# A hybrid decoder step: accumulating decode output, dtx on GpSimd, C's taps a tick later, and paired py and state bursts in the SSD mixer

## The chip, the core and the metric

The kernel runs on one core of a Trainium2 chip. The metric is the device time of one execution in microseconds (us): the median of three runs. The engines are named as the profile names them: PE is TensorE (PEld its weight loads), DVE is VectorE, ACT is ScalarE, POOL is GpSimd, and SP is the queue that issues the transfers.

## What is computed

The reference is one inference step of a trunk of two layers for 256 prompt tokens and 8 decode tokens (one for each of 8 sequences with a state). In each layer three mixers read the same normed input through one input projection, and their outputs go through one output projection. The change lies in the third mixer, the state space one (SSD), with 32 heads of 64 channels, 4 groups of heads and a state of 128 entries per channel:

```
xbc_c, ssm_conv_new = _causal_conv(xbc, ssm_buf, ssm_w, ssm_b)      # 4 taps
xs, bm, cm = split(silu(xbc_c))                                     # x, B, C
dt = softplus(dt + dt_bias); A = -exp(a_log); a = dt * A
# in a chunk of the prompt, per head:
acum = cumsum(a); lmat = exp(acum_i - acum_j) for i >= j, else 0
y = ((C B^T) * lmat * dt_j) x  + (C s) * exp(acum)
s = exp(last) * s + (B * wj)^T x,   wj = exp(last - acum) * dt
# a decode token, per sequence:
s = exp(a) * s + (dt * x) B^T;      y = s C
y = y + d_skip * x
o_ssm = rmsnorm(y * silu(z))
```

The outputs are the two token streams and the new states of all mixers.

## The kernel before

**Tiling.** Channels lie on the 128 partitions and the 264 tokens (`T`: 256 of the prompt, 8 decode) along the free dimension. The SSD channels make 16 channel tiles `ct` of 128 (two heads each); four of them, c = 0 to 3, form a group `g` that shares B and C.

**Projections.** `gemm` (lines 162 to 215) multiplies the weights with the activations. Weights come from memory in pieces of 128 x 1024, four pieces to a projection of 256 columns. Each piece is split into a high part `whi` (ScalarE, line 136) and a low part `wlo` (VectorE, line 129), and each 128 x 128 block is used in three matmuls (line 211): whi with the high and the low activations, wlo with the high ones. So a piece is 24 matmuls and a projection 96. `issue` (line 120) makes the parts ahead of their use, and issues the loads up to six pieces ahead.

**The order of the work.** The order on every compute engine is the order of the program. The small work of the mixers is written as generators. `start` puts one in a list, and `tick` (line 148), called after each piece of a projection, lets every generator in the list run to its next `yield`, the older ones first. A tick is thus as long as 24 matmuls and what the generators add on PE. `yield n` sleeps n ticks. Beside it there is a list `weave`: what is put there runs between the steps of an `in_turn` (line 326) when that has one chain left, otherwise at the end of the tick.

**A group.** `group` (line 652) makes B and C of a group: it fills two tiles from PSUM, starts the convolution on ScalarE (`tap0`), empties the weave, runs the six remaining taps of B and C in turn in one tick on VectorE (lines 663 and 323), then tanh and `cv_silu`, the transposes and the spreading of B and C of the decode tokens over the partitions (`bb`, `cc`).

**A channel tile.** `ssd` (line 691) does one `ct`. Counting its ticks from 0: (0) it loads the decode state `st` (128 x 8 x 128) and evacuates x and z; (1) tap 0 and the gate's tanh; (2) three taps, and half of the states' decay on ScalarE; (3) tanh, gate, the other half; (4) `cv_silu`, `dtx` = x dt for the 8 decode tokens on VectorE (line 719), and the decay matrices `lm` on ScalarE; (5) half of the outer products dtx B into `u` on ScalarE (line 738); (6) the transposes of x, the other half, and the products `lm` x CB, put into the weave; (7) `xdt` (its tile is `vt`, line 749), `xw` (`kt`), the new state st + u (line 752) and its store; (8) PE's burst `py` (lines 757 and 760), and u = st x cc (line 761); (9) PE's burst `pn` for the new prompt state (line 765), y of the prompt (line 768), and the decode output `yd` as the reduction of u (line 770); (10) the copy of pn, stored for each second tile, y of the decode tokens, and the product with the gate on GpSimd (line 778); (12) and (13) the high and low parts of y (lines 781 and 788) and its square, summed up on GpSimd (line 790). As a projection has four ticks, three or four tiles are in flight at a time.

**Buffers.** `tl(tag, shape, bufs)` takes the next of `bufs` buffers of a tag and waits for its last reader. Tags are shared among stages: `x`, `gate` and `lm` have 3 buffers, `sq` has 5, `u` has 1.

Of the kernel before, what the change touches and what calls it, by code (L numbers as in the profile page):

```python
# [19 lines left out]
NB = 8  # L20
# [13 lines left out]
def hybrid_step(ctx, tc, a, depth=DEPTH):  # L34
# [304 lines left out]
    def layer(l, last, ssq_in, between, sq_in):  # L339
# [24 lines left out]
        so = {}  # L364
# [29 lines left out]
        def ret_qk(h, d, psq, psk):  # L394
# [10 lines left out]
            for ps, tag in ((psq, "conv"), (psk, "x")):  # L405
                x1 = tl(tag, [128, T], 3 if tag == "x" else 2)
# [19 lines left out]
            d["pp"] = pp = tl("lm", [128, 384], 3)  # L426
# [7 lines left out]
        def ret_vg(h, d, psv, psg):  # L434
            v = tl("x", [128, T], 3)
# [5 lines left out]
            gate = tl("gate", [128, T], 3)  # L441
# [34 lines left out]
            on = tl("lm", [128, 3, 128], 3)  # L476
# [19 lines left out]
        def sc_prep(c, d):  # L496
            d["ext"] = ext = tl("x", [128, W], 3)
# [17 lines left out]
        def sc_b(c, d, slot, psbg, psg):  # L515
# [5 lines left out]
            gate = tl("gate", [128, T], 3)  # L521
# [6 lines left out]
            m = tl("og", [128, T], 2)  # L528
# [25 lines left out]
        def dt_path(pdt):  # L554
# [10 lines left out]
            rl = tl("x", [128, T], 3)  # L565
# [6 lines left out]
            s1 = tl("x", [128, T], 3)  # L572
# [46 lines left out]
            ac = tl("lm", [128, 384], 3)[32:64, :256]  # L619
# [12 lines left out]
        def cv_prep(ct, tag="x", bufs=3):  # L632
# [19 lines left out]
        def group(g, d, eb, ec, psb, psc):  # L652
# [38 lines left out]
        def ssd(ct, d, ext, psx, psz, ssq):  # L691
# [14 lines left out]
            gate = tl("gate", [128, T], 3)  # L706
# [12 lines left out]
            V.tensor_mul(dtx, xd, dex[:, ct, 0:NB])  # L719
            lms = []  # L720
            for hh in range(2):
                h = 2 * ct + hh
                lm = tl("lm", [128, 384], 3)
# [28 lines left out]
            V.tensor_add(st, st, u)  # L752
            nc.sync.dma_start(a["ssm_state_out"][l, ct], st)
            yield
            py = psm()
            for hh in range(2):
                PE.matmul(py[64 * hh:64 * hh + 64, :256].rearrange("p (b i) -> p b i", b=2), xdt[:, 0, hh],  # L757
                          lms[hh].rearrange("p (b i) -> p b i", b=3)[:, 0:3:2], start=True, stop=False)
            for hh in range(2):
                PE.matmul(py[64 * hh:64 * hh + 64, 128:256], xdt[:, 1, hh], lms[hh][:, 128:256], start=False, stop=True)  # L760
            V.tensor_mul(u, st, d["cc"])
            yield
            pn = psm()
            for j in range(2):
                PE.matmul(pn[:, :128], xw[:, j].rearrange("p h c -> p (h c)"), d["bt"][:, j], start=(j == 0), stop=(j == 1))  # L765
# [4 lines left out]
            V.tensor_reduce(yd, u, axis=mybir.AxisListType.X, op=ALU.add)  # L770
# [11 lines left out]
            if ct:  # L782
                sq = tl("sq", [128, T], 5)
# [95 lines left out]
        for tag, bufs, n in (("st", 3, 3), ("st", 3, 3), ("st", 3, 3), ("bc0", 1, 3), ("bc1", 1, 3), ("gate", 3, 1)):  # L879
# [6 lines left out]
        def evac_a(c, pss, hurry=False):  # L886
            for i, ps in enumerate(pss):
                for j in range(2):
# [7 lines left out]
                    sq = tl("sq", [128, T], 5)  # L896
# [79 lines left out]
    def feed(l, dst, scaled, update, sums=None):  # L976
# [14 lines left out]
        def square(ct):  # L991
            x = acc[:, ct]
            if update:
                squares[ct] = tl("sq", [128, T], 5)
# [3 lines left out]
            else:  # L998
                sq = tl("sq", [128, T], 5)
# [234 lines left out]
```

## Time and profile before

| what | value |
|---|---|
| median of 3 runs (lowest to highest) | 1759.31 us (1759.02 to 1759.42) |
| the profiled execution | 1760.18 us, its span 1758.4 us |
| granted PE clock | 0.999 of full speed |
| first layer's SSD stage, 94.9 to 358.0 us of the span | PE 260.09 us of 263.10, DVE 248.59, ACT 225.22, POOL 69.96 |

The span runs from the first to the last instruction; the profiled execution's own time holds a little more. Busy times count the time in which at least one instruction of an engine is under way. Matmuls overlap, so what one costs is read from the starts of two neighbours, not from its duration. In a timeline row stand the start, the duration, the engine and line, the operation, the tile written and the tiles read, the shape and how many neighbouring instructions the row merges; in square brackets stands the idle time just before it and what ended it. In a row of a group of instructions stand the shapes and the count, then the busy time in us, the mean of one in ns, and the idle time before them.

### The profile page before, as it was taken

The page shows a single profiled execution, that of the slowest core. Times are in us where ns is not written, and L with a number is a line of the kernel's source. Part 1 is how long each engine was busy: PE and PEld are TensorE (multiplying, and loading weights), DVE is VectorE, ACT ScalarE, POOL GpSimd, SP SyncE. Part 2 cuts the span into 40 slices and gives each one's busy share as a digit, 9 for nine tenths or more (in the row PEclk, how much of TensorE's full clock was granted, in tenths as well). Part 3 has the DMA queues.
Part 4 walks back from the last instruction along what each step waited for, and adds up shares of the span by engine and source line. Part 5 has one row for each costly group of instructions (what it writes and reads, how often), then busy time and mean ns, then how long its engine had stood idle before and what let it go on. Part 6 is the DMA issues. An engine that isn't in the chain of part 4 may idle for free.

```text
span 1758.4 us, 36846 instructions
## 1 busy us (share of the span) xinstructions
PE 1735.6 (99%) x14364; PEld 1705.7 (97%) x14364; DVE 1332.2 (76%) x2410; ACT 1010.0 (57%) x1976; POOL 333.5 (19%) x478
## 2 busy tenths in 40 slices
PE   8999999999999999999999999999999999999997
PEld 8999999999999999999999999999999999999997
DVE  7889999974588787554588999999646788765554
ACT  6488888843344444444565888888434444444453
POOL 4213233220021021101202133222102111111022
PEclk9999999999999999999999999999999999999999
DMA  7677787776676766555566777787656777666553
GB/s 276 219 247 249 239 270 249 259 231 180 192 224 210 232 224 211 179 187 180 181 190 212 258 251 241 264 259 247 218 181 186 226 232 218 215 210 183 185 180 104
DMA packets 115487, 382.34 MB, mean 217 GB/s; under 512 B 13872, under 2 KB 21104, under 8 KB 115312
## 3 DMA queue, kind: packets, MB, share of 16 engines
q1 hardware_dynamic: 114880, 378.91, 67.7%
q8 instruction: 112, 1.84, 0.4%
q10 hardware_dynamic: 432, 1.08, 0.2%
q14 instruction: 63, 0.52, 0.1%
HBM read 346.29 MB, written 33.64 MB: 216 GB/s over the span
## 4 chain that ended last, share of the span: by engine, by line
PE 94%; DVE 4%; DMA 1%; issue 1%; ACT 0%; SPq 0%; DVEq 0%; ACTq 0%
PE pj L211 86%; DVE wlo L129 1%; PE m L211 1%; PE m L757 1%; PE m L312 1%; PE m L765 1%; PE m L464 1%; DVE yd L770 0%; DVE conv L323 0%; PE m L422 0%; PE m L760 0%; PE m L482 0%; DVE acc L949 0%; PE pj L386 0%; DMA acc<-x 0%
## 5 line engine op out<-in xcount | busy, mean ns | idle before, releaser
L129 DVE TENSOR_TENSOR wlo<-raw,whi 128x1024 fp32r<-128x1024 f32 x544 | 678.4, 1248 | 321.7 <-issue 160.1
L136 ACT CAST whi<-raw 128x1024 fp32r<-128x1024 f32 x543 | 567.4, 1045 | 601.5 <-PE pj L211 527.7
L211 PE MATMUL pj<-hhi,whi 128*128 128x264 f32 x3256 | 835.9, 290 | 6.5 <-ACT whi L1036 6.0
L211 PE MATMUL pj<-hlo,whi 128*128 128x264 f32 x3256 | 813.2, 286 | 0.0
L211 PEld LDWEIGHTS pj<-hhi,whi 128*128 128x128 f32 x3256 | 613.8, 189 | 17.7 <-issue 6.6
L211 PEld LDWEIGHTS pj<-hlo,whi 128*128 128x128 f32 x3256 | 613.2, 189 | 0.1
L211 PE MATMUL pj<-hhi,wlo 128*128 128x264 f32 x3256 | 485.8, 285 | 0.0
L211 PEld LDWEIGHTS pj<-hhi,wlo 128*128 128x128 f32 x3256 | 433.5, 189 | 0.0
L211 PE MATMUL pj<-mh,whi 128*128 128x264 f32 x1024 | 256.5, 285 | 0.0
L211 PE MATMUL pj<-ml,whi 128*128 128x264 f32 x1024 | 255.8, 285 | 0.0
L211 PEld LDWEIGHTS pj<-mh,whi 128*128 128x128 f32 x1024 | 192.8, 188 | 0.4 <-ACT whi L136 0.3
L211 PEld LDWEIGHTS pj<-ml,whi 128*128 128x128 f32 x1024 | 193.0, 188 | 0.1
L211 PE MATMUL pj<-mh,wlo 128*128 128x264 f32 x1024 | 149.3, 284 | 0.0
L211 PEld LDWEIGHTS pj<-mh,wlo 128*128 128x128 f32 x1024 | 135.0, 188 | 0.0
L738 ACT ACTIVATE u<-bc,dtx 128x128 f32<-128x128 f32 x256 | 82.0, 392 | 37.0 <-DVE yd L770 37.0
L414 POOL TENSOR_TENSOR conv<-conv,rope 128x264 f32<-128x264 f32 x16 | 12.1, 759 | 437.5 <-DVE rope L410 396.4
L702 ACT ACTIVATE st<-st,dex 128x128 f32<-128x128 f32 x256 | 81.2, 389 | 0.0
L323 DVE SCALAR_TENSOR_TENSOR conv<-x,par,conv 128x288 f32<-128x288 f32 (+1 forms) x128 | 68.4, 534 | 14.7 <-ACT conv L317 13.7
L790 POOL TENSOR_TENSOR ssq<-ssq,sq 128x264 f32<-128x264 f32 x30 | 45.3, 1511 | 163.1 <-ACT sq L784 138.6
L903 POOL TENSOR_TENSOR ssq<-ssq,sq 128x264 f32<-128x264 f32 x28 | 30.4, 1086 | 157.4 <-ACT sq L897 157.2
L778 POOL TENSOR_TENSOR og<-og,gate 128x264 f32<-128x264 f32 x32 | 32.2, 1006 | 101.9 <-DVE og L777 95.3
L509 POOL COPY scst<-x 128x16 f32<-128x16 f32 x16 | 13.4, 839 | 190.0 <-DVE x L507 146.4
(314 smaller groups left out, 1665.9 us busy)
## 6 DMA issues: line engine op xcount, KB each, us to landing
raw<-w_in SPq DMA_DIRECT2D x415, 512.0 KB
raw<-w_out SPq DMA_DIRECT2D x128, 512.0 KB
st<-ssm_state SPq DMA_DIRECT2D x32, 512.0 KB
bc<-rows SPq DMA_DIRECT2D x32, 512.0 KB
ssm_state_out<-st SPq DMA_DIRECT2D x32, 512.0 KB
abc<-acum SPq DMA_DIRECT2D x32, 256.0 KB
st<-ret_state SPq DMA_DIRECT2D x16, 512.0 KB
ret_state_out<-st SPq DMA_DIRECT2D x16, 512.0 KB
```

Source lines behind the costliest of these rows:

```text
L129: V.tensor_sub(lo, raw, hi.bitcast(F32))
L136: S.copy(hi, loaded[p])
L211: PE.matmul(ps[gi][c][:, :T], w[:, kk, c * 128:c * 128 + 128], r[half], start=(w is hi and half == 0 and kk + q == 0), stop=(q == 3 and kk ...
L312: PE.transpose(pt[:, j * 128:j * 128 + 128], src[:, j * 128:j * 128 + 128], ident)
L323: V.scalar_tensor_tensor(o[:, :n], ext[:, j:j + n], par[:, c:c + 1], o[:, :n], op0=ALU.mult, op1=ALU.add)
L464: PE.matmul(pd[p0:p0 + 32, :128], qm[:, b], st[:, b], start=(b < 4), stop=(b >= 4))
L702: S.activation(st[:, b], st[:, b], AF.Copy, scale=dex[:, ct, NB + b:NB + b + 1])
L738: S.activation(u[:, b], d["bb"][:, b], AF.Copy, scale=dtx[:, b:b + 1])
L757: PE.matmul(py[64 * hh:64 * hh + 64, :256].rearrange("p (b i) -> p b i", b=2), xdt[:, 0, hh], lms[hh].rearrange("p (b i) -> p b i", b=3)[: ...
L778: G.tensor_mul(y, y, gate)
L790: G.tensor_add(ssq, ssq, sq)
L903: G.tensor_add(ssq2, ssq2, sq)
```

## The change

It does five things.

- **Decode output.** The multiply of 128 x 1024 (line 761) and the reduction (line 770) become eight `scalar_tensor_tensor`, one for each decode token, 128 x 128 each, that multiply the state with cc and put the sum of the products into a column of `yd` through `accum_out`. Four are in tick 8 and four in tick 9.
- **New state.** The addition st + u and the store go into the weave of tick 7.
- **dtx** goes from VectorE to GpSimd.
- **Pairs.** An even tile keeps its `xdt`, `xw` and `lm`. The odd tile that follows runs py for both into one PSUM tile, and a tick later pn for both into another, which one copy evacuates. The even tile's y and what follows it come four ticks later.
- **C's taps.** `group` runs B's taps in one tick, with the weave between them, and C's taps in the next, beside B's tanh; C's tanh goes a tick later. The loop that empties the weave first is gone.

Buffers go with it: `x`, `gate` and `lm` get 4 buffers, `sq` 2. The product `m` of the short convolution moves from `og` to `lm`, and two of three squares that the second layer's first projection reads move from `sq` to `lm`.

```diff
         def group(g, d, eb, ec, psb, psc):
...
             yield
-            while weave:
-                woven()
-            in_turn(taps(ob, eb, 288, 4, P_SW, 16 + g, 24, par), taps(oc, ec, 288, 4, P_SW, 20 + g, 24, par))
+            in_turn(taps(ob, eb, 288, 4, P_SW, 16 + g, 24, par))
             B, C = eb, ec
             yield
             S.activation(B[:, :288], ob[:, :288], AF.Tanh)
+            in_turn(taps(oc, ec, 288, 4, P_SW, 20 + g, 24, par))
+            yield
             S.activation(C[:, :288], oc[:, :288], AF.Tanh)
-            yield
             cv_silu(B, ob)
...
             dtx = tl("dtx", [128, NB], 2)
-            V.tensor_mul(dtx, xd, dex[:, ct, 0:NB])
+            G.tensor_mul(dtx, xd, dex[:, ct, 0:NB])
...
-            V.tensor_add(st, st, u)
-            nc.sync.dma_start(a["ssm_state_out"][l, ct], st)
-            yield
-            py = psm()
-            for hh in range(2):
-                PE.matmul(py[64 * hh:64 * hh + 64, :256].rearrange("p (b i) -> p b i", b=2), xdt[:, 0, hh],
-                          lms[hh].rearrange("p (b i) -> p b i", b=3)[:, 0:3:2], start=True, stop=False)
-            for hh in range(2):
-                PE.matmul(py[64 * hh:64 * hh + 64, 128:256], xdt[:, 1, hh], lms[hh][:, 128:256], start=False, stop=True)
-            V.tensor_mul(u, st, d["cc"])
-            yield
-            pn = psm()
-            for j in range(2):
-                PE.matmul(pn[:, :128], xw[:, j].rearrange("p h c -> p (h c)"), d["bt"][:, j], start=(j == 0), stop=(j == 1))
+
+            def new_state():
+                V.tensor_add(st, st, u)
+                nc.sync.dma_start(a["ssm_state_out"][l, ct], st)
+
+            weave.append(new_state)
+            yield
+            pair.append((xdt, xw, lms))
+            if ct % 2:
+                both = psm()
+                for i, (xt, _, ls) in enumerate(pair):
+                    pi = both[:, 256 * i:256 * i + 256]
+                    for hh in range(2):
+                        PE.matmul(pi[64 * hh:64 * hh + 64].rearrange("p (b i) -> p b i", b=2), xt[:, 0, hh],
+                                  ls[hh].rearrange("p (b i) -> p b i", b=3)[:, 0:3:2], start=True, stop=False)
+                    for hh in range(2):
+                        PE.matmul(pi[64 * hh:64 * hh + 64, 128:256], xt[:, 1, hh], ls[hh][:, 128:256], start=False, stop=True)
+                pys[ct - 1], pys[ct] = both[:, :256], both[:, 256:]
+            yd = tl("yd", [128, NB], 2)
+
+            def decode(bs):
+                for b in bs:
+                    V.scalar_tensor_tensor(u[:, b], st[:, b], 1.0, d["cc"][:, b], op0=ALU.mult, op1=ALU.mult,
+                                           accum_out=yd[:, b:b + 1])
+
+            decode(range(0, 4))
+            yield
+            if ct % 2:
+                pn = psm()
+                for i, (_, xs, _) in enumerate(pair):
+                    for j in range(2):
+                        PE.matmul(pn[:, 128 * i:128 * i + 128], xs[:, j].rearrange("p h c -> p (h c)"), d["bt"][:, j],
+                                  start=(j == 0), stop=(j == 1))
+                pair.clear()
+            decode(range(4, NB))
+            if ct % 2 == 0:
+                yield 4
             y = tl("og", [128, T], 2)
             dsk = par[:, P_DSK + ct:P_DSK + ct + 1]
-            V.scalar_tensor_tensor(y[:, :TP], x[:, :TP], dsk, py[:, :TP], op0=ALU.mult, op1=ALU.add)
-            yd = tl("yd", [128, NB], 2)
-            V.tensor_reduce(yd, u, axis=mybir.AxisListType.X, op=ALU.add)
-            yield
-            if ct % 2 == 0:
-                so[0] = tl("so", [128, 2, 128], 2)
-            S.copy(so[0][:, ct % 2], pn[:, :128])
-            if ct % 2 == 1:
-                nc.sync.dma_start(a["ssm_new"][l, ct // 2], so[0])
+            V.scalar_tensor_tensor(y[:, :TP], x[:, :TP], dsk, pys.pop(ct), op0=ALU.mult, op1=ALU.add)
+            yield
+            if ct % 2:
+                so = tl("so", [128, 2, 128], 2)
+                S.copy(so.rearrange("p j n -> p (j n)"), pn[:, :256])
+                nc.sync.dma_start(a["ssm_new"][l, ct // 2], so)
             V.scalar_tensor_tensor(y[:, TP:T], xd, dsk, yd, op0=ALU.mult, op1=ALU.add)
             G.tensor_mul(y, y, gate)
```

More of the change, by code (lines that the diff above doesn't have):

```diff
@@ L362, in hr @@
             return hhi[:, k], hlo[:, k]
-        so = {}
+        pair, pys = [], {}
         rot_t = []
@@ L425, in ret_qk @@
             yield
-            d["pp"] = pp = tl("lm", [128, 384], 3)
+            d["pp"] = pp = tl("lm", [128, 384], 4)
             V.tensor_mul(pp[:, :256], psc[:, :256], dm)
@@ L434, in ret_vg @@
         def ret_vg(h, d, psv, psg):
-            v = tl("x", [128, T], 3)
+            v = tl("x", [128, T], 4)
             V.tensor_mul(v, psv[:, :T], r2)
@@ L440, in ret_vg @@
             st, kt, pp, qm = d["st"], d["kt"], d["pp"], d["qm"]
-            gate = tl("gate", [128, T], 3)
+            gate = tl("gate", [128, T], 4)
             S.activation(gate, pre, AF.Tanh, scale=0.5)
@@ L475, in ret_vg @@
             yield
-            on = tl("lm", [128, 3, 128], 3)
+            on = tl("lm", [128, 3, 128], 4)
             for j in range(3):
@@ L496, in sc_prep @@
         def sc_prep(c, d):
-            d["ext"] = ext = tl("x", [128, W], 3)
+            d["ext"] = ext = tl("x", [128, W], 4)
             G.memset(ext[:, 0:2], 0.0)
@@ L520, in sc_b @@
             yield
-            gate = tl("gate", [128, T], 3)
+            gate = tl("gate", [128, T], 4)
             S.activation(gate, pre, AF.Tanh, scale=0.5)
@@ L527, in sc_b @@
             cv = d["cv"]
-            m = tl("og", [128, T], 2)
+            m = tl("lm", [128, 384], 4)[:, :T]
             G.tensor_mul(m[:, :TP], cv[:, :TP], bg[:, :TP])
@@ L564, in dt_path @@
             dtb = par[:, P_DTB:P_DTB + 1]
-            rl = tl("x", [128, T], 3)
+            rl = tl("x", [128, T], 4)
             S.activation(rl, d0, AF.Relu, bias=dtb)
@@ L571, in dt_path @@
             yield
-            s1 = tl("x", [128, T], 3)
+            s1 = tl("x", [128, T], 4)
             V.tensor_scalar(s1, d0, 2.0, None, op0=ALU.add)
@@ L618, in dt_path @@
             yield
-            ac = tl("lm", [128, 384], 3)[32:64, :256]
+            ac = tl("lm", [128, 384], 4)[32:64, :256]
             V.tensor_copy(ac, pa[32:64, :256])
@@ L705, in ssd @@
             o = tap0(ext, 288, P_SW, ct, P_SB, par)
-            gate = tl("gate", [128, T], 3)
+            gate = tl("gate", [128, T], 4)
             S.activation(gate, pre, AF.Tanh, scale=0.5)
@@ L722, in ssd @@
                 h = 2 * ct + hh
-                lm = tl("lm", [128, 384], 3)
+                lm = tl("lm", [128, 384], 4)
                 ab = abc_t[ct][:, hh]
@@ L782, in ssd @@
             if ct:
-                sq = tl("sq", [128, T], 5)
+                sq = tl("sq", [128, T], 2)
                 S.activation(sq, y, AF.Square)
@@ L878, in layer @@
         xres, xparts = [], []
-        for tag, bufs, n in (("st", 3, 3), ("st", 3, 3), ("st", 3, 3), ("bc0", 1, 3), ("bc1", 1, 3), ("gate", 3, 1)):
+        for tag, bufs, n in (("st", 3, 3), ("st", 3, 3), ("st", 3, 3), ("bc0", 1, 3), ("bc1", 1, 3), ("gate", 4, 1)):
             t = tl(tag, [128, n, T], bufs)
@@ L895, in evac_a @@
                         yield
-                    sq = tl("sq", [128, T], 5)
+                    sq = tl("sq", [128, T], 2)
                     S.activation(sq, acc[:, ct], AF.Square)
@@ L993, in square @@
             if update:
-                squares[ct] = tl("sq", [128, T], 5)
+                squares[ct] = tl("sq", [128, T], 2) if ct % 3 == 2 else tl("lm", [128, 384], 4)[:, :T]
                 S.activation(squares[ct], x, AF.Square)
@@ L998, in square @@
             else:
-                sq = tl("sq", [128, T], 5)
+                sq = tl("sq", [128, T], 2)
                 S.activation(sq, x, AF.Square)
```

4 lines of the change are left out of this document (2 added, 2 removed).

## The prediction

> **What bounds the kernel now.** I read the page first, then the list of waits of TensorE, then its timeline around the SSD bursts, then VectorE in the same stretch.
>
> ```profile
> span 1758.4 us, 36846 instructions
> PE 1735.6 (99%) x14364; PEld 1705.7 (97%) x14364; DVE 1332.2 (76%) x2410; ACT 1010.0 (57%) x1976; POOL 333.5 (19%) x478
> DVE  7889999974588787554588999999646788765554
> PE m L757 <- DVE vt L749: 6.1, 6, 1.6
> PE pj L211 <- ACT whi L1036: 6.0, 2, 5.7
> 172.90:240.90 68.00, 66.78 (x548) 64.77 (x548) 64.85 (x111) 58.31 (x149) 19.50 (x32) 1.00 0.76 251
> ```
>
> The first rows are the page, the next two the list of waits (total, times, longest), the last one the windows view of one SSD group: 68.00 us with PE 66.78, the second weight column, DVE 64.85, ACT 58.31, POOL 19.50. TensorE has work 99% of the time. The only waits that it has inside the work are six for `vt` (line 749), 6.1 us in all; the 6.0 us for `whi` are the start of the program, which the change leaves alone. VectorE, 76% on average, is at nine tenths in the SSD stages (slices 3 to 7 and again later): 64.85 of 68.00. So TensorE sets the time, and in the SSD stage VectorE stands right behind it. Two things can be won: TensorE's own cost of the small bursts, and the 6.1 us.
>
> ```profile
> 312.49 0.28 PE L211 MATMUL pj<-hlo,whi 128*128 128x264 f32 x1
> 312.61 0.65 PE L211 MATMUL pj<-hhi,wlo 128*128 128x264 f32 x4
> 313.18 0.65 PE L757 MATMUL m<-lm,vt 128*64 128x256 f32 x4
> 313.67 0.39 PE L760 MATMUL m<-lm,vt 128*64 128x128 f32 x4
> 313.98 0.39 PE L211 MATMUL pj<-hhi,whi 128*128 128x264 f32 x1
> 314.21 0.29 PE L211 MATMUL pj<-hlo,whi 128*128 128x264 f32 x1
> ...
> 316.05 1.13 PE L211 MATMUL pj<-hhi,wlo 128*128 128x264 f32 x8
> 317.02 0.60 PE L765 MATMUL m<-bt,kt 128*128 128x128 f32 x4
> 317.38 0.37 PE L211 MATMUL pj<-hhi,whi 128*128 128x264 f32 x1
> 317.59 0.29 PE L211 MATMUL pj<-hlo,whi 128*128 128x264 f32 x1
> ```
>
> Durations overlap here, so starts count. A projection matmul takes 0.122 us from start to start (312.49 to 312.61).
>
> **py in pairs.** The four wlo matmuls from 312.61 would be over at 313.10, and the stream is back in step at 314.21, one interval after 314.09: a py burst costs 0.99 us. Its inside, 313.18 to 313.98, is 0.80. The other 0.19 is going in (0.08) and coming out (0.11), and is paid once for two tiles instead of twice. 32 bursts become 16: 16 x 0.19 = 3.0 us. The pairs hold nothing back that TensorE needs, so this lies on the path.
>
> **New states in pairs.** Eight wlo matmuls from 316.05 end at 317.03; in step again at 317.59 - 0.12 = 317.47, so one pn burst costs 0.44.
>
> ```profile
> 1745.26 0.61 PE L386 MATMUL pj<-cvst 128*128 128x128 f32 x4
> 1745.71 0.61 PE L386 MATMUL pj<-ml,mh 128*128 128x128 f32 x4
> ```
>
> Four such matmuls amid others take 0.45 (1745.26 to 1745.71). Behind the projections the weight loads are hidden, in a long burst they are not. I take nothing; the bounds are 0 and the 0.09 of coming out (317.38 to 317.59, less 0.12), 1.4 us for 16.
>
> **Where the 6.1 us come from.**
>
> ```profile
> 174.44 0.42 DVE L749 TENSOR_TENSOR vt<-m,tok 128x256 f32<-128x256 f32 x1
> 177.47 0.65 PE L757 MATMUL m<-lm,vt 128*64 128x256 f32 x4
> 188.18 0.41 DVE L749 TENSOR_TENSOR vt<-m,tok 128x256 f32<-128x256 f32 x1
> 188.52 0.41 DVE L751 TENSOR_TENSOR kt<-m,wj 128x256 f32<-128x256 f32 x1
> 188.85 1.21 DVE L752 TENSOR_TENSOR st<-st,u 128x1024 f32<-128x1024 f32 x1
> 189.98 0.42 DVE L714 SCALAR_TENSOR_TENSOR gate<-gate,pre 128x264 f32<-128x264 f32 x1
> 190.86 0.65 PE L757 MATMUL m<-lm,vt 128*64 128x256 f32 x4
> 215.63 0.51 DVE L323 SCALAR_TENSOR_TENSOR conv<-B,par,conv 128x288 f32<-128x288 f32 x1
> 216.06 0.51 DVE L323 SCALAR_TENSOR_TENSOR conv<-C,par,conv 128x288 f32<-128x288 f32 x1
> 218.48 0.42 DVE L749 TENSOR_TENSOR vt<-m,tok 128x256 f32<-128x256 f32 x1
> 218.95 0.65 PE L757 MATMUL m<-lm,vt 128*64 128x256 f32 x4 [1.22 <-DVE vt L749]
> ```
>
> These are `vt` on VectorE and the burst that reads it, for channel tiles c=0, 1 and 3 of one group. VectorE's lead, end of `vt` to burst, is 2.61 us at c=0 and gone at c=3, where TensorE waits 1.22: from c=0 to 1 VectorE needs 13.74 (174.44 to 188.18) where TensorE needs 13.39, and from c=1 to 3 it needs 30.30 where TensorE, its wait aside, needs about 26.8, because the next group's six taps, 0.43 each (215.63 to 216.06), stand in front of c=3's `vt`. The list's longest wait is 1.6. I count four of the six as of this kind; the two that close a layer's stage are small and have no group behind them.
>
> **C's taps a tick later.** Three taps, 3 x 0.43 = 1.29 us, go behind the last tile's `vt`. The tanh of C goes a tick later too, but `cv_silu` of C stays where it was, with VectorE between, so nothing downstream moves.
>
> **VectorE's work per tile.** Out: `mul` and `reduce`.
>
> ```profile
> L761 DVE TENSOR_TENSOR u<-st,bc 128x1024 f32<-128x1024 f32 x32 | 39.0, 1218 | 0.0
> L770 DVE TENSOR_REDUCE yd<-u 128x8 f32<-128x1024 f32 x32 | 38.8, 1212 | 0.0
> L719 DVE TENSOR_TENSOR dtx<-x,dex 128x8 f32<-128x8 f32 x32 | 11.5, 358 | 1.1
> L738 ACT ACTIVATE u<-bc,dtx 128x128 f32<-128x128 f32 x256 | 82.0, 392 | 37.0 <-DVE yd L770 37.0
> L530 POOL TENSOR_TENSOR og<-conv,rope 128x8 f32<-128x8 f32 x16 | 9.2, 574 | 0.0
> 496.82 0.27 DVE L470 BATCH_NORM_STATS2 bs<-m 128x6 f32<-128x128 f32 x1
> 497.12 0.18 DVE L471 BATCH_NORM_AGGREGATE mv<-bs 128x2 f32<-128x6 f32 x1
> 497.22 0.27 DVE L470 BATCH_NORM_STATS2 bs<-m 128x6 f32<-128x128 f32 x1
> ```
>
> A 1024-wide operation takes 1.13 from start to start (188.85 to 189.98), so the pair frees 2 x 1.135 = 2.27. In come eight 128-wide multiplies with a sum on the side; the trace has no such instruction. Below, its price is that of width alone: 0.34 at 256 (188.18 to 188.52) and 1.13 at 1024 give 1.03 ns per element, so 0.20 at 128, 1.6 for eight. Above, it is the statistics row and the small operation that collects its result, 0.30 + 0.10 = 0.40 (496.82 to 497.22), 3.2 for eight. It cannot be below the width. I take 0.27, 2.16 for eight: the sum has to be written out by something, but no step waits for another's result as the aggregate does, so it is nearer the lower row. The gain is then 0.11.
>
> The Trainium skill, "VectorE: DVE Perf Modes", section "Two Vector instructions with no wait between them", says that an operation which also writes out its accumulator is two instructions, the main one and a read; no run here shows it yet. By it the two instructions become sixteen, and its "Rules for kernel authors" ask for few operations; without the read the 0.20 would hold and the time be that of the full gain below. The same rules call `tensor_reduce` the slowest VectorE operation; this trace disagrees, 1212 ns against 1218 for the multiply.
>
> `dtx` leaves VectorE: 0.36 by its row, of which part is the wait for what it follows; I take 0.3 (bounds 0 and 0.36). On GpSimd it costs about the 0.57 of the 128x8 row. GpSimd is in order, and while it waits for `cv_silu` the keep-copies, the gate product and the sum of squares stand behind it; TensorE needs none of these within several ticks. ScalarE's outer products need dtx, but sit idle 37.0 us for `yd` already, 1.2 us for each of the 32 tiles, and those waits cover the 0.57. With that cover gone it would be 0.57 per tile on ScalarE, which has 9.7 us free per group.
>
> So VectorE wins d = 0.3 + 0.11 = 0.41 per tile, with the bounds 0.97 (at 0.20) and -0.63 (at 0.40).
>
> **What is late next.** With pairs, TensorE's way from c=0 to the burst at c=1 loses one py and one pn: 13.39 - 0.99 - 0.44 = 11.96. From c=1's burst to c=3's it is 26.78 - 0.19 = 26.59. VectorE needs 13.74 - d and 30.30 - 1.29 - 2d. The lead at c=3 is 2.61 - (1.78 - d) - (2.42 - 2d) = -1.59 + 3d, which at d = 0.41 is -0.36. A wait of 0.36 stays where 1.22 was: 0.86 saved, at four places 3.4 us. The two small waits I leave.
>
> **Moved at no cost.** The state's addition and its store go to the weave, behind the next tile's gate product or between C's taps: at most 1.29 + 0.34 later. SP is in order and the weight loads stand behind that store, but they are issued six pieces ahead, 6 x 24 x 0.122 = 17.6 us; without that cover it would be up to 1.6 per tile. The even tile's y goes four ticks later, next to the odd one's; the odd one, which the output projection needs last, stays. Fewer `sq` buffers let the squares run less far ahead of GpSimd's sums at the start, where ScalarE waits 2.99 us for TensorE to free `whi` anyway:
>
> ```profile
> 32.09 1.05 ACT L136 CAST whi<-raw 128x1024 fp32r<-128x1024 f32 x1 [2.99 <-PE pj L211]
> ```
>
> Without that cover it would be about 1 us, once. The wider pools only lift waits.
>
> **Sum.** 3.0 + 0 + 3.4 = 6.4 us. The profiled execution took 1760.18 us, 1.78 around its span and 0.87 above the median; the saving taken from the median gives 1759.31 - 6.4 = 1752.9. About 0.2%, 3.5 us, can be told from no change, so faster means below 1755.8.
>
> **Rivals.**
> - The full gain: at 0.20 per step the lead stays positive, all 6.1 go and 3.0 with them: 1759.3 - 9.1 = 1750.2. For it speaks that the eight steps are independent; against, that a sum must be stored.
> - Slower: each accumulating step holds VectorE until its sum is out, as the statistics pair. At 0.40, d = -0.63, the lead at c=3 is -3.5, 2.3 us more wait than now in each of about six groups: 6 x 2.3 - 3.0 = +10.8, 1770. It decides from 0.32 per step (six times 0.5 eats the 3.0). For it speaks that VectorE has only 3.15 us free per group; against, that no semaphore stands between the step and its read.
> - The saving moves: the faster even tiles put VectorE 1.43 us behind before each double burst, or the steps cost about 0.31. Then 3.0 is won in the bursts and given back as `vt` waits at c=1 and c=3: 1757 to 1761, no change.
>
> **How the numbers follow.** Forecast 0.45, full gain 0.15, no change 0.17, slower 0.23. Faster by over 0.2% is 0.60. The range from 1749.5 to 1766 holds the first three cases and the nearer half of the slower one (0.36 per step gives d = -0.31, lead -2.5, 6 x 1.3 - 3.0 = +4.8, 1764). The first two cases alone span 1749.5 to 1755.8.
>
> **What would show it.** The bursts: py of two tiles within 1.8 us, 16 of them. The waits of TensorE for `vt`: four of 0 to 0.7 us, none at c=0 or c=1. The decode steps: start to start 0.27. VectorE's busy time per group some 1.6 us lower. Wrong it would be if `vt` waits total over 6 us, if the steps stand 0.32 or more apart, or if TensorE waits for `wlo` or for the mix tiles.

## The result, and the profile after

| kernel | median | lowest to highest | executions |
|---|---|---|---|
| before | 1759.37 us | 1759.02 to 1760.04 | 4 |
| after | 1749.22 us | 1748.12 to 1751.07 | 4 |

The ratio is 0.9942, with a 95% interval from 0.9929 to 0.9954: 10.15 us faster, where 6.4 was forecast, and 0.3 us below the lower end of the range. The profiled execution of after took 1748.12 us, its span 1746.4, at a granted clock of 0.998. Executions in which the chip was disturbed are left out of all medians below; that takes one from each of two kernels, e12 and e8, and e8's is the one with the trace, so e8 is read by its times alone.

The page of after:

```profile
span 1746.4 us, 37289 instructions
PE 1728.2 (99%) x14364; PEld 1702.7 (98%) x14364; DVE 1318.4 (75%) x2826; ACT 1010.3 (58%) x1960; POOL 318.2 (18%) x510
DVE  7889999964587787554588999999646788775554
```

The rows of TensorE in its list of waits (total, times, longest):

```profile
PE pj L211 <- ACT whi L1055: 5.6, 1, 5.6
PE m L764 <- DVE vt L748: 1.8, 4, 0.6
```

TensorE still sets the time. Its waits for `vt` fell from 6.1 us in six to 1.8 in four. VectorE still stands at nine tenths in the SSD stages, though it does less. The windows view of after for the first layer's SSD stage, which now runs from 93.4 to 351.4 (columns: length, then busy time of PE, weight loads, DVE, ACT, POOL):

```profile
93.40:351.40 258.00, 257.04 (x2131) 251.37 (x2130) 241.38 (x616) 225.22 (x563) 60.43 (x129) 1.00 0.79 258
```

It holds the same 2131 TensorE instructions as the 263.10 us of before. DVE went from 248.59 to 241.38, so by 1.8 us per group. That is about half of what left it: counting only the time that each instruction adds to the engine's busy time, the decode output takes 8.8 us less in this stage and `dtx` 5.7, and part of that comes back because rows of other operations are longer (under e4).

**Where the 10 us are.** Number the projection matmuls in order in both traces and compare their starts. The 400th, ahead of the first SSD stage, is 1.5 us earlier in after; the 2700th, behind that stage, 6.6; the 6900th, ahead of the second layer's, 6.8; the 9200th, behind it, 11.8. So each SSD stage gained 5.0, and what lies behind them hardly anything. The 1.5 at the start is no part of the change: two more executions of it, below, have 0.5 and 0.3 there, with 9.3 and 10.0 in the two stages together.

**Half of it is the bursts of py.** The timeline of TensorE in after:

```profile
186.45 0.65 PE L211 MATMUL pj<-hhi,wlo 128*128 128x264 f32 x4
187.02 0.65 PE L764 MATMUL m<-lm,vt 128*64 128x256 f32 x4
187.50 0.39 PE L767 MATMUL m<-lm,vt 128*64 128x128 f32 x4
187.72 0.60 PE L764 MATMUL m<-lm,vt 128*64 128x256 f32 x4
188.15 0.39 PE L767 MATMUL m<-lm,vt 128*64 128x128 f32 x4
188.47 0.39 PE L211 MATMUL pj<-hhi,whi 128*128 128x264 f32 x1
188.70 0.29 PE L211 MATMUL pj<-hlo,whi 128*128 128x264 f32 x1
...
190.51 1.14 PE L211 MATMUL pj<-hhi,wlo 128*128 128x264 f32 x8
191.48 1.05 PE L782 MATMUL m<-bt,kt 128*128 128x128 f32 x8
192.29 0.37 PE L211 MATMUL pj<-hhi,whi 128*128 128x264 f32 x1
192.50 0.28 PE L211 MATMUL pj<-hlo,whi 128*128 128x264 f32 x1
```

Read as the prediction reads them: the four wlo matmuls would be over at 186.94, and the stream is in step again at 188.70 - 0.12 = 188.58, so two tiles cost 1.64 us where twice 0.99 stood. That saves 0.33 or 0.34 in each of 16 bursts, 5.3 us; going in and coming out were to give 0.19. The rest is inside: from start to start, the first four of a tile take 0.48 and its last four, ahead of another tile, 0.22; the second tile's take 0.43 and 0.32. Together 1.45, against twice 0.80. The new states save nothing: 191.49 to 192.38 is 0.89, twice 0.44.

**The other half is the waits,** 4.3 us by the list. What is left of them is of one form, here in TensorE's timeline of after at the last tile of the third group:

```profile
278.97 0.65 PE L764 MATMUL m<-lm,vt 128*64 128x256 f32 x4
279.46 0.39 PE L767 MATMUL m<-lm,vt 128*64 128x128 f32 x4
280.16 0.65 PE L764 MATMUL m<-lm,vt 128*64 128x256 f32 x4 [0.32 <-DVE vt L748]
```

VectorE's timeline beside it:

```profile
279.69 0.42 DVE L748 TENSOR_TENSOR vt<-m,tok 128x256 f32<-128x256 f32 x1
```

The double burst starts while `vt` of the odd tile (279.69 to 280.11) is still being made: the even tile's half, 0.7 us, is a head start, and the wait of 0.32 stands between the halves. The other one of this layer is its last tile, 0.6; the second layer has the same two.

**The decode steps.** VectorE's timeline of after:

```profile
201.88 0.28 DVE L773 SCALAR_TENSOR_TENSOR u<-st,bc 128x128 f32<-128x128 f32 x1
202.09 0.07 DVE L773 DVE_READ_ACCUMULATOR u<-st,bc 128x1 f32 x1
202.09 0.28 DVE L773 SCALAR_TENSOR_TENSOR u<-st,bc 128x128 f32<-128x128 f32 x1
```

The groups of the new lines (count, busy us, mean ns, idle before):

```profile
L773 DVE DVE_READ_ACCUMULATOR u<-st,bc 128x1 f32 x256 | 20.5, 80 | 0.0
L718 POOL TENSOR_TENSOR dtx<-x,dex 128x8 f32<-128x8 f32 x32 | 6.6, 205 | 272.7 <-DVE x L647 272.7
```

Each step does bring a read of the accumulator, 256 of them in all, but the read starts together with the next multiply (202.09), and the steps stand 0.21 us apart. Eight cost 1.70 where multiply and reduction cost 2.27. `dtx` takes 0.205 on GpSimd.

### The profile page after: what moved, and what is told of

It reads as the page before. It is cut to its first block, busy times and chain, and to the rows that moved or that the text cites. A ratio compares the mean times of both kernels' runs of the same rounds, so it can differ in the third digit from the quotient of the medians.

```text
span 1746.4 us, 37289 instructions
## 1 busy us (share of the span) xinstructions
PE 1728.2 (99%) x14364; PEld 1702.7 (98%) x14364; DVE 1318.4 (75%) x2826; ACT 1010.3 (58%) x1960; POOL 318.2 (18%) x510
## 5 line engine op out<-in xcount | busy, mean ns | idle before, releaser
L737 ACT ACTIVATE u<-bc,dtx 128x128 f32<-128x128 f32 x256 | 81.8, 391 | 20.7 <-DVE u L773 20.4
L323 DVE SCALAR_TENSOR_TENSOR conv<-x,par,conv 128x288 f32<-128x288 f32 (+1 forms) x128 | 72.4, 566 | 13.9 <-issue 6.8
L922 POOL TENSOR_TENSOR ssq<-ssq,sq 128x264 f32<-128x264 f32 x28 | 30.4, 1087 | 157.3 <-ACT sq L916 157.2
L773 DVE SCALAR_TENSOR_TENSOR u<-st,bc 128x128 f32<-128x128 f32 x256 | 58.9, 284 | 0.0
L718 POOL TENSOR_TENSOR dtx<-x,dex 128x8 f32<-128x8 f32 x32 | 6.6, 205 | 272.7 <-DVE x L647 272.7
```

The costliest lines, as they stand in the source:

```text
L323: V.scalar_tensor_tensor(o[:, :n], ext[:, j:j + n], par[:, c:c + 1], o[:, :n], op0=ALU.mult, op1=ALU.add)
L718: G.tensor_mul(dtx, xd, dex[:, ct, 0:NB])
L737: S.activation(u[:, b], d["bb"][:, b], AF.Copy, scale=dtx[:, b:b + 1])
L773: V.scalar_tensor_tensor(u[:, b], st[:, b], 1.0, d["cc"][:, b], op0=ALU.mult, op1=ALU.mult, accum_out=yd[:, b:b + 1])
L922: G.tensor_add(ssq2, ssq2, sq)
```

## The experiments

The theory after the result: the pairs give 5.3 us in TensorE's bursts; the cheap steps, and `dtx` off VectorE, give the lead that ends most waits; pairing takes lead away, so the first gain leans on the second. The rivals: the pairs or C's taps do all of it, or the steps don't matter. On four chips the kernel before took 1759.48, 1759.24, 1760.27 and 1759.70 us (medians); kernels with one such number were run together. "By stages" is the gain of both SSD stages, found as above.

### The parts one by one (before: 1759.48)

**e0.** The change, unaltered:

> The change once more, as the base for the others of this round. If 1.5 us of the 12.0 us between the two spans belong to the start of one execution (the difference is there before the SSD stage begins), the median is 9.5 to 10.5 us below the kernel before; if the start is part of the change, each execution shows it and the spread is small.

1751.01 us (1749.90 to 1751.68), 0.9952 [0.9939, 0.9964]; by stages 9.3; waits for `vt` 2.7.

**e2.** The decode output as multiply and reduction again, all else as changed:

```
-            decode(range(0, 4))
+            V.tensor_mul(u, st, d["cc"])
...
-            decode(range(4, NB))
+            V.tensor_reduce(yd, u, axis=mybir.AxisListType.X, op=ALU.add)
```

> The decode output by multiply and reduce again, the rest as changed. Theory: VectorE has 2.27 us per tile instead of 8 x 0.21 = 1.70, so 0.57 more per tile and 1.7 more between c=0 and c=3: 4 to 9 us slower than the change, waits for vt at 6 to 10 us. Rival (the decode steps are off the path): 0 to 1 us slower.

1765.43 us (1764.70 to 1766.52), 1.0033 [1.0021, 1.0045]: slower than before the change, and 14.4 us slower than the change, where I expected 4 to 9. From its list of waits:

```profile
PE m L764 <- DVE vt L748: 11.1, 11, 1.6
PE pj L211 <- DVE wlo L129: 4.4, 6, 0.8
```

The double bursts are there as in after, but against their 5.3 us stand 15.5 of waits for VectorE, at `vt` and, for the first time, at `wlo`. VectorE has 32 x 0.57 = 18.2 us more to do than with the steps, and 14.4 of them show (16.2 by stages). So without the accumulating steps the rest of the change loses 6 us. The list accounts for 4 of them: 15.5 of waits, less the 6.1 of before and the 5.3 of the bursts.

**e4.** Single bursts again, each tile with its own py and pn, in the ticks of the kernel after:

```
-            if ct % 2:
-                both = psm()
-                for i, (xt, _, ls) in enumerate(pair):
...
+            py = psm()
+            for hh in range(2):
...
-            if ct % 2 == 0:
-                yield 4
```

> py and pn of each tile in its own ticks again, the rest as changed. Theory (a pair of py costs 1.65 us where two cost 1.98): 16 x 0.33 = 5.3 us slower than the change by the bursts, the waits for vt within 2 us of the change's 1.9. Rival (only going in and coming out is saved, 0.19, and the rest comes from the waits): 3 us slower by the bursts.

1751.29 us (1750.72 to 1751.70), 0.9954 [0.9941, 0.9966]; by stages 7.3; no wait for `vt` is left. Beside the change's 1751.01 the pairs seem to be worth nothing: most of what the bursts save comes back as waits, and, by stages, 2.0 stay.

The pairs also cost VectorE work. `ml`, the low part of y, has these rows in the tile view (shortest, median and longest in ns) before the change and after it:

```profile
L292 DVE SCALAR_TENSOR_TENSOR ml<-og,par,mh x32: 479/484/493, 127.4 to 1240.1; 128x264 fp32r<-128x264 f32 x32
L292 DVE SCALAR_TENSOR_TENSOR ml<-og,par,mh x32: 478/481/987, 138.7 to 1229.1; 128x264 fp32r<-128x264 f32 x32
```

In the change 11 of the 32 take 0.98 us in place of 0.48, the same 11 in all three of its traces, all of even tiles. Each of them starts while GpSimd adds up squares (`ssq`), and none of the other 21 does. With single bursts, as before the change, none is longer than 0.50. So 5.5 us of VectorE's work come from where the pairs put the even tile's y. Of the products `lm` x CB, 8 of 64 take 1.11 us in place of 0.55, 4.5 us in all; before the change none does. These come with the steps alone (p1, below) and without them (e2) too, so no single part brings them. What these 10 us cost in the time was not tried.

**e1.** C's taps beside B's again, in one tick, with the weave emptied first:

```
-            in_turn(taps(ob, eb, 288, 4, P_SW, 16 + g, 24, par))
+            while weave:
+                woven()
+            in_turn(taps(ob, ...), taps(oc, ec, 288, 4, P_SW, 20 + g, 24, par))
...
             S.activation(B[:, :288], ob[:, :288], AF.Tanh)
-            in_turn(taps(oc, ec, 288, 4, P_SW, 20 + g, 24, par))
-            yield
             S.activation(C[:, :288], oc[:, :288], AF.Tanh)
+            yield
```

> C's taps back in B's tick, the rest as changed. Theory (every piece of VectorE's relief counts, since vt of the last tile of a group comes with 0 to 1 us of lead): three taps, 1.29 us, come before vt of the last tile again, at six places with -0.3 to 2.3 us of lead: 2 to 5 us slower than the change, TensorE's waits for vt at 4 to 7 us in place of 1.9. Rival (the rest of the relief and the double burst would have been enough): 0 to 1 us slower, waits below 2.5 us.

1746.09 us (1745.61 to 1749.63), 0.9928 [0.9915, 0.9940]; by stages 12.5, and no wait for `vt` at all. I expected a loss; it is 4.9 us faster than the change on the same chip. So this part of the change costs time, and the theory falls in this point. 12.5 is about all that there was to win: 5.3 in the bursts and the 6.1 of waits; the last 1.1 is not placed.

### The steps alone, and what dtx and the pairs are worth (before: 1759.24)

**p1.** The kernel before, with only the accumulating steps put in:

```
-            V.tensor_mul(u, st, d["cc"])
...
+            decode(range(0, 4))
...
-            V.tensor_reduce(yd, u, axis=mybir.AxisListType.X, op=ALU.add)
+            decode(range(4, NB))
```

> The kernel before with nothing but the accumulating decode steps (0.21 us from start to start, as the changed kernel's trace shows, in place of 2.27 per tile). Theory (0.57 us less on VectorE per tile is what lifts the waits for vt): at the last tile of a group vt comes 1.7 us earlier, which is more than the 1.2 to 1.6 us that TensorE waits there: all 6 us of waits go, 1752 to 1754. Rival (the taps or the double burst lifted the waits): the waits stay above 3 us, 1756 to 1759.

1753.69 us (1752.92 to 1755.86), 0.9966 [0.9954, 0.9979]; by stages 6.4; no wait for `vt`. 0.57 us less VectorE work per tile is enough to end all 6.1 us of waits when the bursts are single.

**e10.** As e1, and `dtx` on VectorE again:

```
-            G.tensor_mul(dtx, xd, dex[:, ct, 0:NB])
+            V.tensor_mul(dtx, xd, dex[:, ct, 0:NB])
```

> C's taps beside B's, as the fastest run so far, with dtx back on VectorE. Theory (0.2 to 0.36 us per tile on VectorE, 1 us at the last tile of a group, where the lead is 0.1 to 0.9 us plus the 0.7 us of the even tile's half of the burst): waits for vt of 0 to 2 us come back, 0 to 3 us slower than 1746. Rival (GpSimd delays the outer products by more than VectorE gains): faster by up to 2 us.

1753.38 us (1750.45 to 1755.13), 0.9961 [0.9949, 0.9974]; by stages 7.5; five waits for `vt`, 3.7 us. Against the same kernel with `dtx` on GpSimd this is 5 us by stages and 6 by the ratios (the two ran on different chips), where I expected 0 to 3. VectorE's timeline shows the price:

```profile
203.39 1.00 DVE L647 SCALAR_TENSOR_TENSOR x<-x,conv 128x288 f32<-128x288 f32 x1
204.43 0.17 DVE L719 TENSOR_TENSOR dtx<-x,dex 128x8 f32<-128x8 f32 x1
204.51 0.42 DVE L639 TENSOR_TENSOR B<-pj,r 128x256 f32<-128x256 f32 x1
```

The operation starts 0.04 after the end of what it reads, where others start some 0.08 before the end of their predecessor, and it takes 0.08 itself from start to start: 0.2 in this place. In three of the 32 tiles `dtx` takes 0.60 us and so 0.65 in its place, in the others 0.17 as here. That is some 7.7 us of VectorE work in all.

**e8.** The edits of e1 and e4 together:

> Single bursts and C's taps beside B's, the rest as changed (decode steps, dtx on GpSimd, the state's addition in the weave, the buffers). Theory (the pair saves 0.33 us on TensorE at 16 places, and with C's taps beside B's nothing of it goes into waits): 5 us slower than the run with C's taps beside B's and paired bursts, so 1750 to 1752, with no waits for vt. Rival (C's taps beside B's is what makes that run fast, whatever the bursts): within 2 us of its 1746.

1751.8 us (1750.68 to 1753.91), 0.9956 [0.9942, 0.9969]. Against 0.9928 with double bursts, the pairs are here worth some 5 us, their full 5.3: e1 has no wait that could take it back.

**e11.** C's taps later, as changed, but the weave emptied ahead of B's:

```
             yield
+            while weave:
+                woven()
             in_turn(taps(ob, eb, 288, 4, P_SW, 16 + g, 24, par))
```

> The changed kernel, C's taps still a tick later, but the weave emptied ahead of B's taps as before the change. Theory A (ScalarE, in order, stands 2.0 us at C's tanh at each group's start, behind C's late taps, and is late for the next tile from there): as the change, 1749 to 1751, with that wait still 2 us. Theory B (VectorE stands 0.9 us at B's first tap, with the products in the weave behind it): 3 to 5 us faster than the change, as with the taps together.

1748.28 us (1746.55 to 1749.78), 0.9932 [0.9918, 0.9945]; by stages 11.4; one wait for `vt`, 1.1, in the stage in which ScalarE's outer products stood 1.9 for a transfer of `rows`.

### Order in the burst, one burst for all, and twice the steps (before: 1760.27)

**e9.** As e1, and pn of two tiles directly behind py of two tiles:

```
                 pys[ct - 1], pys[ct] = both[:, :256], both[:, 256:]
+                pn = psm()
+                for i, (_, xs, _) in enumerate(pair):
...
             decode(range(0, 4))
             yield
-            if ct % 2:
-                pn = psm()
```

> C's taps beside B's, and the new states of a pair in the same burst as its py, so that TensorE leaves and re-enters the projections once per pair instead of twice. Theory (coming out of a burst costs about 0.1 us each time, and TensorE has no waits left in that version): 1 to 2.5 us faster than 1746, if kt is there in time; kt comes 0.3 us after vt, so up to 0.3 us of new waits at four places. Rival (a burst of eight state matmuls costs 0.89 us, twice the 0.44 of four, so it has no cost of its own to save): within 1 us of 1746.

1746.88 us (1745.66 to 1747.91), 0.9924 [0.9910, 0.9938]; by stages 12.5, as with two bursts. TensorE's timeline there:

```profile
187.65 0.65 PE L211 MATMUL pj<-hhi,wlo 128*128 128x264 f32 x4
...
189.67 1.16 PE L773 MATMUL m<-bt,kt 128*128 128x128 f32 x8
190.59 0.37 PE L211 MATMUL pj<-hhi,whi 128*128 128x264 f32 x1
190.79 0.28 PE L211 MATMUL pj<-hlo,whi 128*128 128x264 f32 x1
```

From 188.14 to 190.67 is 2.53 us, the sum of 1.64 and 0.89. The state matmuls have no cost of entry that could be shared, also not with py.

**e5.** The change with the odd tile's half first:

```
-                for i, (xt, _, ls) in enumerate(pair):
+                for i, (xt, _, ls) in reversed(list(enumerate(pair))):
```

> The changed kernel with the odd tile's py first in the burst. Theory (the even tile's half, 0.7 us, is a head start for the odd tile's vt): waits for vt begin 0.7 us earlier at the four places where they are, and at those with less than 0.7 us of lead: waits of 4 to 6 us in place of 1.9 to 2.7, 2 to 4 us slower than the change. Rival (the lead is made up elsewhere): 0 to 1 us.

1750.59 us (1749.81 to 1752.96), 0.9947 [0.9935, 0.9960]; by stages 7.7; waits for `vt` 4.7 in five. The waits grew by 2 to 3 us in the trace, as they must if the even half is a head start; in the medians this lies within the spread of the change itself.

**e7.** Each accumulating step twice, which adds work and leaves the output as it is:

```
                     V.scalar_tensor_tensor(u[:, b], st[:, b], 1.0, ..., accum_out=yd[:, b:b + 1])
+                    V.scalar_tensor_tensor(u[:, b], st[:, b], 1.0, ..., accum_out=yd[:, b:b + 1])
```

> The changed kernel with each accumulating step done twice (the output is the same), so that a step costs VectorE 0.42 us in effect, about the 0.40 at which the prediction's slower rival was priced. That rival: 1770, from waits for vt at each odd tile. Theory (VectorE then has 1.7 us more per tile, some 69 us of work in a group for which TensorE needs 66): VectorE-bound stages, 1770 to 1790, with waits for vt and for wlo. Other rival (VectorE's order is not on the path): below 1755.

1829.96 us (1829.34 to 1830.52), 1.0396 [1.0382, 1.0410], where I expected 1770 to 1790. VectorE's timeline:

```profile
202.40 0.29 DVE L773 SCALAR_TENSOR_TENSOR u<-st,bc 128x128 f32<-128x128 f32 x1
202.61 0.08 DVE L773 DVE_READ_ACCUMULATOR u<-st,bc 128x1 f32 x1
202.73 0.29 DVE L775 SCALAR_TENSOR_TENSOR u<-st,bc 128x128 f32<-128x128 f32 x1
202.94 0.28 DVE L773 SCALAR_TENSOR_TENSOR u<-st,bc 128x128 f32<-128x128 f32 x1
...
204.59 0.45 DVE L647 SCALAR_TENSOR_TENSOR x<-x,conv 128x288 f32<-128x288 f32 x1
```

From the list of waits:

```profile
PE pj L211 <- DVE wlo L129: 26.0, 20, 2.4
PE m L764 <- DVE vt L748: 14.3, 11, 1.9
PE m L312 <- DVE x L647: 13.9, 14, 1.3
```

The second of a pair writes the same places as the first and starts only after its read: 0.33 apart, then 0.21 to the next. Four pairs take 2.19 (202.40 to 204.59), so 0.55 each, 0.335 more than a single step: for 256 that is 86 us of VectorE work. The kernel is some 80 us slower than the change (1.0396 less 0.9942 of 1759). Past the point where VectorE is the slower one, its work passes almost one to one into the time. Not all of the 80 need be VectorE's: TensorE's waits for it come to 58.7 us in the list (4.2 more for `C` and 0.3 for `rope`), and its granted clock is 0.98 in the SSD stages, where it is 1.00 in after. What the clock costs was not parted from the rest.

### What C's taps cost (before: 1759.70)

In e1 two things differ from the change at once, and each has a place in the traces where it could cost. VectorE's timeline in after, at the start of a group:

```profile
207.33 1.21 DVE L129 TENSOR_TENSOR wlo<-raw,whi 128x1024 fp32r<-128x1024 f32 x1
209.41 0.52 DVE L323 SCALAR_TENSOR_TENSOR conv<-B,par,conv 128x288 f32<-128x288 f32 x1 [0.86 <-issue]
209.84 0.55 DVE L743 TENSOR_TENSOR lm<-lm,cb 128x384 f32<-128x384 f32 x1
```

and in e1:

```profile
207.31 1.22 DVE L129 TENSOR_TENSOR wlo<-raw,whi 128x1024 fp32r<-128x1024 f32 x1
208.45 1.02 DVE L744 TENSOR_TENSOR lm<-lm,cb 128x384 f32<-128x384 f32 x2
209.39 0.52 DVE L323 SCALAR_TENSOR_TENSOR conv<-B,par,conv 128x288 f32<-128x288 f32 x1
```

Theory B: in both, B's first tap starts at 209.4, 0.1 after the end of tap 0 on ScalarE (209.31 and 209.29). With the weave first, the products `lm` x CB fill that time; without it, VectorE stands for 0.86 with the products queued behind the tap. Theory A is on ScalarE. Its timeline in after:

```profile
216.18 0.45 ACT L667 ACTIVATE C<-conv 128x288 f32<-128x288 f32 x1 [2.01 <-DVE conv L323]
```

and in e1:

```profile
212.78 0.43 ACT L666 ACTIVATE B<-conv 128x288 f32<-128x288 f32 x1
213.12 0.43 ACT L667 ACTIVATE C<-conv 128x288 f32<-128x288 f32 x1
```

C's tanh now waits 2.0 us for the late taps, and the splitting of weights and all else on ScalarE stands behind it. To part the two, all four combinations ran on one chip; the missing one, **e12**, has the taps together and the weave behind them; **e13** is e1, **e14** is e11 and **e15** the change:

```
-            in_turn(taps(ob, eb, 288, 4, P_SW, 16 + g, 24, par))
+            in_turn(taps(ob, ...), taps(oc, ec, 288, 4, P_SW, 20 + g, 24, par))
...
-            in_turn(taps(oc, ec, 288, 4, P_SW, 20 + g, 24, par))
-            yield
...
+            yield
```

> C's taps beside B's, but without emptying the weave ahead of them: VectorE meets B's first tap, which waits for ScalarE's tap 0, with the products of the weave behind it. Theory B (that 0.9 us stand of VectorE per group is what the change's new order loses): 3 to 5 us slower than with the weave first, as the change, about 1750. Theory A (C's late tanh holds ScalarE): as with the weave first, about 1746, since no tanh is late here.

> The version with the weave first and the taps together once more, beside the others of this round: 1745.5 to 1747.5, no waits for vt.

> The version with the weave first and C's taps a tick later once more. Theory B: within 1 us of the run with the taps together. Theory A, or both: 1.5 to 4 us slower than that.

> The change once more, as the fourth corner: 1749 to 1751. Theories A and B together: the sum of the two losses over the run with the taps together.

| | weave behind B's first tap | weave first |
|---|---|---|
| C's taps a tick later | 1749.17 (the change), by stages 10.0 | 1748.20, by stages 11.5 |
| C's taps beside B's | 1749.44, by stages 8.5 | 1746.52, by stages 12.8 |

The ratios are 0.9941 [0.9929, 0.9952] and 0.9938 [0.9926, 0.9950] in the first row, 0.9942 [0.9929, 0.9955] and 0.9928 [0.9916, 0.9939] in the second. Emptying the weave first is worth 2.9 us with the taps together and 1.0 with C's later. C's taps a tick later cost 1.7 with the weave first, and give 0.3 (1.5 by stages) with the weave behind. So B alone costs 2.9, A alone 1.7, and both together 2.7: they do not add up. TensorE's waits for `vt` go the same way: 3.4 us with B alone (e12), 1.1 with A alone (e14), 2.0 with both (e15) and none with neither (e13). By stages the 2.9 is 4.3 and the 1.7 is 1.3 (1.1 between e11 and e1); the 1.0 and the 0.3 are near what the medians can tell. That it is ScalarE's stand that takes the 1.7 is the reading of the rows above (in the list of waits of the first stage it is 6.0 us in after, 4.0 in e11, and absent in e1); it was not tried alone.

The best kernel of the case is thus the change without its part on C's taps: 1746.09 and 1746.52 us, 4.9 and 2.7 less than the change on the same chips.

## Why the prediction was right and wrong

- **The bursts of py: the largest error of size.** 3.0 us were forecast, 5.3 came. The failed step is "Its inside, 313.18 to 313.98, is 0.80. The other 0.19 is going in (0.08) and coming out (0.11)": what stays inside is not 0.80 for each. The first four matmuls of a tile cost 0.48 when projections stand ahead and 0.43 when another tile does; the last four 0.31 when projections follow and 0.22 when another tile does. So 0.15 of the burst's boundaries lay within what I took as its inside. With 5.3 in the place of 3.0 the prediction's sum is 8.7 and its time 1750.6. That the measured 1749.22 lies below the range comes from this term first; the last 0.3 us are less than the change moves from chip to chip, where it was 10.2, 8.5 and 10.5 us faster. The rival of full gain, 9.1, comes nearest, but by luck: its terms are 3.0 and 6.1 where 5.3 and 4.3 came.
- **New states: right.** 0 was taken from 0 to 1.4. The row of four fp32 matmuls amid others, 0.45, was the one to go by. That the weight loads show in a long burst is not seen: eight cost 0.89, twice 0.44.
- **The step's price: wrong, to the good side.** 0.27 was taken between 0.20 and 0.40, and 0.21 came. That is the width alone: the two rows that were rounded to 0.20 give 0.208. The statistics pair that set the upper end has an operation that reads the result of the one before; the accumulating steps depend on nothing of each other, and their reads run beside the next multiply. Where the second of two steps writes what the first wrote, 0.33 is seen (e7). The Trainium skill, "VectorE: DVE Perf Modes", section "Two Vector instructions with no wait between them", counts such an operation as two instructions, and the trace agrees, with 256 reads of 80 ns; but sixteen instructions took 1.70 us where two had taken 2.27, so here their number was not what decided.
- **dtx: near in size, misread in kind.** 0.36 was taken for one price with a wait in it. It is the mean of two kinds: in before, 18 of the 32 take 0.17 us, and 14 take 0.60. Each of the 14 starts while GpSimd adds up squares and ends 0.02 to 0.03 behind that:

```profile
193.08 0.60 DVE L719 TENSOR_TENSOR dtx<-x,dex 128x8 f32<-128x8 f32 x1
192.70 0.95 POOL L790 TENSOR_TENSOR ssq<-ssq,sq 128x264 f32<-128x264 f32 x1 [7.32 <-ACT sq L784]
```

  With 0.2 in the place of the short ones and 0.64 in that of the long ones, VectorE was freed of 0.39 per tile, where 0.3 was taken. The 0.57 for GpSimd is such a mean too: ten of the 16 operations in that row take 0.20 to 0.21 and six 1.19, each of the six beside VectorE's `wlo`. The cover held: ScalarE's outer products wait for `u` 20.4 us in all, and never for `dtx`. What the move is worth in the time, 5 to 6 us, could not be seen from its size alone.
- **The waits: right in sum, by two errors that cancel.** 3.4 us were to be saved, and the list shows 4.3 in the profiled execution, and 3.4 and 4.1 in two others (e0, e15). With 0.57 + 0.3 = 0.87 for d, the prediction's own formula, -1.59 + 3d, gives a lead of 1.02 at c=3 and no wait at all, as in the rival of full gain. The waits stayed because of the next point; the longer rows of `ml` and `lm` work the same way. And they stayed in other places: I left the two small waits that close a layer's stage, 0.21 and 0.31 us before, and they grew to 0.65 and 0.58, while the two of the second group went and the two of the third fell from 1.58 to 0.32 and 0.30.
- **C's taps a tick later: the sign failed.** The step was "Three taps, 3 x 0.43 = 1.29 us, go behind the last tile's `vt` ... so nothing downstream moves". Two things moved: VectorE stands 0.86 at B's first tap, since the products no longer run ahead of it, and ScalarE stands 2.0 at C's tanh. I had listed the loop that empties the weave as gone, but asked only what it delays, not what it fills. And the 1.29 us are not won but lent: they stand behind `vt` of c=3, ahead of everything of the next group. With the weave first, the lead at c=3 of the first group is 3.00 when C's taps come later (e11) and 1.87 when they do not (e1); at the next c=1 it is 3.38 against 2.94, and 3.40 in the second execution of the latter (e13).
- **Where the waits are.** "four of 0 to 0.7 us, none at c=0 or c=1" came true by the letter. But the formula gave the same lead at each group's end, and the traces show one that is used up. The lead of `vt`, from its end to the start of its own half of the double burst, for the odd tiles of the first layer (c=1 and c=3 of four groups), worked out from the starts and durations of the timelines; 0.05 is a half that waited, or just did not:

```
after:                  3.92 2.31 | 2.68 0.90 | 1.30 0.05 | 0.51 0.05
taps together (e1):     3.91 1.87 | 2.94 0.78 | 1.99 0.06 | 1.89 0.61
```

  In after, VectorE loses 1.2, 1.4 and 0.8 us from one group's c=1 to the next; with the taps together 1.0, 1.0 and 0.1. The loss varies: e13, the latter kernel again, has leads of 3.88, 3.40, 3.01 and 2.38 at c=1. So waits come only from the third group on, when the reserve of the stage's start is gone. The 0.7 us of the even tile's half are part of this lead; the prediction counted to the start of the burst and left them out.
- **Moved at no cost: held in part.** SP's order and the squares gave TensorE no wait, and its wait for `whi` at the start of the program is 5.6 us (6.4 and 5.5 in the two further traces), where it was 6.0. But the even tile's y, moved next to the odd one's, makes 11 rows of `ml` twice as long, 5.5 us of VectorE's work that the prediction put at nothing.
- **The slower rival: priced far too low.** It gave +10.8 us at 0.40 per step and put the turn at 0.32. The changes of the work were measured instead: 18.2 us more on VectorE cost 14.4 (e2), and 86 cost 80 (e7). The step from 0.21 to 0.40 is 49 us of work, so by these two rates an estimate of 39 to 46 us of time, and multiply with reduction, 2.27 for eight or 0.28 per step, is already slower than before. The rival counted the extra wait once for each of six groups from a fresh lead; VectorE, once behind, has none.
- **"The saving moves": seen, where the steps are dear or the weave stands wrong.** With the change's order of the taps, pairs and single bursts differ by 0.3 us in the medians; with the weave first and the taps together, by 5.

## What to carry to other kernels

When two engines are within a few per cent of each other in a stage, work out the lead of the second one at every hand-over through the whole stage: a formula for one group hides that a reserve is being used up, and each saving on the first engine is only worth what the second can follow. Where an order is loosened, ask of each step that moves what it had been filling: an in-order engine that meets its wait earlier stands with ready work queued behind it. Look at the spread of a row before its mean is taken as a price; a mean of two kinds hides what an operation ran beside. And cost a burst by its boundaries, between projections and between its own parts, not as an inside with two ends.

## What the runs showed of the hardware

- The read of VectorE's accumulator (80 ns) starts with the next multiply and adds nothing: 128x128 steps stand 0.21 us apart, and 0.33 when the second writes the same places as the first.
- Eight fp32 matmuls for the new states cost the same in one burst as in two (0.89), and the same behind py as behind projections, while py's matmuls get cheaper next to their like (1.64 for two tiles against 1.98).
- `dtx`, 128x8, takes 0.17 us on VectorE, and 0.60 in the 14 cases of before in which it starts while GpSimd adds two tiles of 128x264. On GpSimd it takes 0.205.
- `ml`, 128x264, takes VectorE 0.48 us, and 0.98 in the 11 cases of after in which it starts while GpSimd does that addition. A GpSimd operation of 128x8 takes 0.2 us by itself and 1.19 beside VectorE's `wlo` (six of 16 in before).
- The start of the program moves by about 1 us between executions of one kernel (ahead of the first SSD stage three executions of the change are 1.5, 0.5 and 0.3 us earlier than the profile before; e11 and its repetition e14 are 1.1 and 1.4 later), so differences of 1 us between single profiles are read by stages.
